# Banded attention: the softmax division moved behind the value products, and cached K and V loaded without a staging copy

## The chip, the cores and the metric

The kernel runs on one core of a Trainium2 chip. The metric is the device time of one execution in microseconds. The core has five engines that run side by side: TensorE (PE in the profile; its weight loads are shown apart as PEld), VectorE (DVE), ScalarE (ACT), GpSimd (POOL) and SyncE (SP), which issues most of the transfers. Transfers (DMAs) run on 16 engines of their own. A matmul writes into PSUM, a memory of eight banks, and DVE or ACT carries the result from there into SBUF.

## The reference

One layer of a hybrid encoder on 2048 tokens of 1024 features, all in float32. A norm and one combined projection give, among others, q, k and v of eight heads of 64 columns. Attention is banded: tokens go in chunks of 64, and a chunk sees itself and the eight chunks before it, with a learned bias by distance:

```python
scores = jnp.einsum('bnqhd,bnkhd->bnhqk', qc, kb).astype(jnp.float32) * (d ** -0.5)
...
scores = jnp.where(valid[None, :, None, None, :], scores + bias[None, None], NEG_INF)
p = jax.nn.softmax(scores, axis=-1)
out = jnp.einsum('bnhqk,bnkhd->bnqhd', p.astype(vb.dtype), vb)
```

Beside it runs a recurrent branch (RWKV-7). Both branches are projected (`proj_a`, `proj_b`), gated, added, projected once more (`w_out`), normed and added to x. A feed-forward part with a squared ReLU follows. The change concerns the attention alone.

## The kernel before, in words

The tokens go through in four groups of 512 (`G`). For each group `run` (L1206) does three stages: the recurrent branch (`phase_rwkv`), the attention (`phase_attention`, L884) and the merge (`phase_merge`, L935), in which gates, branches and `w_out` come together. The feed-forward part follows after all four groups.

Float32 products are made from halves: `split` (L68) rounds a tensor to the reduced format F32R on ACT (`hi`) and takes the remainder on DVE (`lo`), and `mm3` (L72) sums hi·hi, hi·lo and lo·hi. `dense` (L82) does so for a projection of 128 columns: load 512 KB of weights (L62, on SP's queue), split them, 24 matmuls of 512 columns into a PSUM tile `psd`.

`att_pair` (L756) handles two heads at a time, four pairs to a group. It makes q, k and v by three calls of `dense`. Keys stand in `KK`, values in `VV`; each holds two groups of tokens, the group before in half 0 and the own in half 1, since the band reaches back 512 tokens. The own half is stored to device memory (L797, L798) and read again one group later: from the second group on, `kr` and `vr` are loaded (L764, L767) into one staging buffer of their own, and ACT copies them into half 0 of `KK` and `VV` (L765, L768).

Then for each head of the pair (`par`), each half of the 512 queries (`half`) and each 128 queries of that (`b`, number `qb`), one score block:

- PE: scores of 128 queries and up to 640 keys into `ps_s` (L820);
- DVE: add the bias and take the extreme `mn` of each row (L826);
- ACT: exponential of the row, its sum into `sm` (L831; the reading of the sum is an instruction of its own);
- DVE: reciprocal of the sum (L833), and the row multiplied by it (L834);
- PE: up to five transposes of 128x128 into `ps_pt` (L838);
- ACT and DVE: the transposed block split into `PTh` and `PTl` (L842, L843).

After two blocks PE multiplies with the values into a PSUM tile `ps_pv` of 256 columns (L850, 12 matmuls where the whole band exists). The hi and lo parts of V's columns come out on the lower and upper 64 rows; ACT copies the upper rows to `y2` (L852) and DVE adds both into `ya` (L853). When both heads are through, `ya` (128 columns of features by 512 queries) is split into `self.ya` (L856), which the merge multiplies with `proj_a`.

`ps_s` and `ps_pt` have one buffer each of two PSUM banks, `ps_pv` two of one bank each, `psd` two. `KK` and `VV` have two buffers, so that the next pair's projections can be made while this pair's blocks run.

After the four pairs `load_y` (L914) reads the recurrent branch's result, and `branch(y, 1, i)` (L923, called at L908) multiplies it with `proj_b`, gates it (L932) and stores it; the merge does the same with `proj_a`.

The source's order isn't that of the engines. The framework places instructions on each engine by a plan of its own, made when the program is built: what is ready goes first, and among ready ones what stands earlier in the source. On each engine, and on SP's queue of transfers, the order is then fixed. In the trace PE so alternates between score blocks of one pair, projections `psd` of the next, and, in the last pair, the `proj_b` products `ps_p`.

## Time and profile before

| what | value |
|---|---|
| time, median of 3 runs (lowest to highest) | 3462.41 us (3460.87 to 3465.66) |
| time of the profiled execution | 3462.33 us |
| its span, first to last instruction | 3460.6 us |
| mean granted clock of TensorE | 0.985 |
| instructions | 50793 |
| DMA share, 16 engines: main queue | 40.2% |

The profile names an instruction by its line in the kernel, its engine, its operation, and the tiles written and read ("out<-in"). Busy time counts an engine's instructions without overlap twice. A matmul's duration is longer than the step from one to the next, as matmuls are pipelined. "Idle before" is the idle time of an engine just before the instructions of a group, and what ended it. Times in a timeline count from the first instruction.

The attention stages in this execution lie at about 318 to 434, 803 to 950, 1339 to 1486 and 1875 to 2021 us (from the first projections that only attention uses to the last value product); the merges follow each. The first group has no group before it, so its stage has fewer keys, and no `kr` and `vr`.

### The profile page before, as it was taken

The numbers are of one execution on the slowest core, as the hardware profiler recorded it, in microseconds if no ns is written. First come the engines' busy times: TensorE is split into PE (matmuls) and PEld (weight loads), VectorE is DVE, ScalarE is ACT, GpSimd is POOL, SyncE is SP. The second block draws the span as 40 slices with busy tenths as digits, with TensorE's granted clock in tenths as the row PEclk, the third lists the DMA queues.
The fourth block names the chain that finished last, engine by engine and source line by source line (L and its number), as shares of the span: only waits on it lengthen the run. The fifth ranks groups of instructions, "written<-read, shape, count | busy, mean of one in ns | idle before, by whom it ended". The sixth has DMA issues, their size and how long they took to land. (4 is left out here: it accounts for less than half of the span.)

```text
span 3460.6 us, 50793 instructions
## 1 busy us (share of the span) xinstructions
PE 3310.7 (96%) x19233; PEld 2677.4 (77%) x19233; DVE 2421.3 (70%) x4206; ACT 1429.6 (41%) x2399; POOL 352.7 (10%) x700
## 2 busy tenths in 40 slices
PE   7999999999998999999999979999999999999998
PEld 5777777777877777877777867888888878888886
DVE  5774856766856765865774875777887788766667
ACT  4434634436644445644435635333331143331112
POOL 2210002100003110002210000111100021100001
PEclk9999999999999999999999999999999999999999
DMA  5223453225365225365224277334845374343333
GB/s 147 82 86 125 130 182 119 62 89 186 111 223 161 62 92 159 122 226 163 82 86 134 81 232 254 125 120 143 271 175 188 109 239 129 113 152 98 98 98 110
DMA packets 430124, 481.14 MB, mean 139 GB/s; under 512 B 19564, under 2 KB 322864, under 8 KB 429880
## 3 DMA queue, kind: packets, MB, share of 16 engines
q1 hardware_dynamic: 419640, 444.34, 40.2%
q0 software_dynamic: 10240, 33.56, 2.6%
q8 instruction: 151, 2.47, 0.3%
q14 instruction: 93, 0.76, 0.1%
HBM read 356.16 MB, written 124.81 MB: 139 GB/s over the span
## 5 line engine op out<-in xcount | busy, mean ns | idle before, releaser
L78 PE MATMUL ps_dn<-fop 128*128 128x512 f32 x3072 | 700.1, 390 | 0.9 <-DVE u L1169 0.9
L78 PEld LDWEIGHTS ps_dn<-fop 128*128 128x128 f32 x3072 | 575.9, 188 | 121.3 <-DVE u L1169 1.3
L78 PE MATMUL psd<-hh,whi 128*128 128x512 f32 x1344 | 546.4, 407 | 16.7 <-ACT whi L69 13.5
L78 PE MATMUL psd<-hl,whi 128*128 128x512 f32 x1344 | 544.9, 405 | 0.0
L78 PE MATMUL psd<-hh,wlo 128*128 128x512 f32 x1344 | 541.4, 403 | 0.7 <-DVE wlo L70 0.5
L69 ACT CAST whi<-wraw 128x1024 fp32r<-128x1024 f32 (+1 forms) x296 | 255.6, 864 | 578.2 <-PE psd L78 392.3
L70 DVE TENSOR_TENSOR wlo<-wraw,whi 128x1024 fp32r<-128x1024 f32 (+1 forms) x296 | 292.6, 989 | 264.9 <-ACT whi L69 200.4
L1169 DVE TENSOR_TENSOR u<-u,ps_dn 128x512 f32<-128x512 f32 x480 | 322.5, 684 | 152.8 <-PE ps_dn L78 152.0
L78 PEld LDWEIGHTS psd<-hh,whi 128*128 128x128 f32 x1344 | 258.3, 192 | 71.7 <-ACT whi L69 15.5
L78 PEld LDWEIGHTS psd<-hh,wlo 128*128 128x128 f32 x1344 | 258.0, 192 | 52.5 <-DVE wlo L70 3.5
L78 PEld LDWEIGHTS psd<-hl,whi 128*128 128x128 f32 x1344 | 258.6, 192 | 48.8
L69 ACT CAST fop<-wdraw 128x1024 fp32r<-128x1024 f32 x64 | 67.1, 1049 | 427.5 <-DVE u L1169 321.9
L1090 POOL DMA_DIRECT2D ad<-r x128 | 69.4, 543 | 683.8 <-DVE r L1089 683.8
L78 PE MATMUL ps_p<-yh,whi 128*128 128x512 f32 x256 | 107.8, 421 | 29.8 <-DVE th L932 17.8
L69 ACT CAST s12h<-s 128x1024 fp32r<-128x1024 f32 x32 | 33.7, 1054 | 185.1 <-PE ps_u L78 185.1
L826 DVE CUSTOM_DVE_ANT_0 sc<-bias,ps_s 128x640 f32<-128x640 f32 (+4 forms) x128 | 93.3, 729 | 22.4 <-PE ps_pt L838 13.0
L831 ACT ACTIVATE sc<-sc,mn 128x640 f32<-128x640 f32 (+4 forms) x128 | 97.8, 764 | 22.4 <-DVE mn L826 21.7
L78 PE MATMUL ps_p<-yh,wlo 128*128 128x512 f32 x256 | 105.4, 412 | 1.6 <-DVE wlo L70 1.6
L959 PE MATMUL ps_o<-whi,mh 128*128 128x512 f32 x256 | 98.6, 399 | 7.7 <-ACT whi L69 6.8
L78 PE MATMUL ps_p<-yl,whi 128*128 128x512 f32 x256 | 105.3, 412 | 0.0
L843 DVE TENSOR_TENSOR PTl<-ps_pt,PTh 128x640 fp32r<-128x640 f32 (+4 forms) x128 | 94.1, 735 | 12.9 <-ACT PTh L842 12.2
L959 PE MATMUL ps_o<-wlo,mh 128*128 128x512 f32 x256 | 102.1, 399 | 1.1 <-DVE wlo L70 1.1
(345 smaller groups left out, 6566.9 us busy)
## 6 DMA issues: line engine op xcount, KB each, us to landing
wraw<-in_w_in_dram SPq DMA_DIRECT2D x168, 512.0 KB
wraw<-in_w_up_dram SPq DMA_DIRECT2D x80, 512.0 KB
ad<-r POOLq DMA_DIRECT2D x128, 256.0 KB, 2.5
wdraw<-in_w_down_dram SPq DMA_DIRECT2D x64, 512.0 KB
araw<-ad SPq DMA_DIRECT2D x64, 512.0 KB
gd<-gate SPq DMA_DIRECT2D x64, 256.0 KB
th<-gd SPq DMA_DIRECT2D x64, 256.0 KB
wraw<-in_w_out_dram SPq DMA_DIRECT2D x64, 256.0 KB
```

Of the source, the lines that this page charges most:

```text
L69: self.nc.scalar.copy(hi, src)
L70: self.nc.vector.tensor_tensor(lo, src, hi.bitcast(F32), ALU.subtract)
L78: mm = nc.tensor.matmul(ps, l, r, start=n == 0, stop=n == last).ins
L826: nc.vector.tensor_tensor_reduce(sc[:, 0:n], bias[:, s0:640], pss[:, c0 : c0 + n], 1.0, 3.0e38, ALU.add, ALU.min, mn,)
L831: nc.scalar.activation(sc[:, 0:n], sc[:, 0:n], AF.Exp, scale=-1.0, bias=mn, accum_out=sm)
L843: nc.vector.tensor_tensor(lv, pst[:, 0:nk], hv.bitcast(F32), ALU.subtract)
L959: nc.tensor.matmul(ps[t], l[:, k, ts], r[:, 0], start=k == 0 and j == 0, stop=k == KB - 1 and j == 2)
L1090: nc.gpsimd.dma_start(self.ad[fb][:, th], r)
L1169: nc.vector.tensor_tensor(u[t][:, ns], u[t][:, ns], ps, ALU.add)
```

## The change

Three things are done. The cached K and V are loaded straight into half 0 of `KK` and `VV`. The exponentials are transposed and multiplied with V as they are, and their sums are kept, one column for each head and block, in a tile `sm` of 128x8 for a pair. And a new function `finish` divides at the end: reciprocal of the eight columns, a transpose to 8x128 (`ps_rt`), a copy to `rt`, four matmuls with a constant 0/1 matrix `place` that spread each query's two factors over the 64 rows of their heads (`ps_rb`, 128x512), a product with `ya`, and the split. `finish` of a pair stands in the source behind the next pair's projections; that of the last pair stands behind `load_y`. `ps_pv` becomes 512 columns wide, so `y2` and `ya` are made once for a head instead of twice.

```diff
         if not first:
-            kr = ap.tile([P, 2, G], F32, tag="kr", bufs=1, name="kr")
-            nc.sync.dma_start(kr, self.kc[p])
-            nc.scalar.copy(KK[:, :, 0], kr)
-            vr = ap.tile([P, GT, 2, 2, C], F32, tag="kr", bufs=1, name="vr")
-            nc.sync.dma_start(vr, self.vc[p])
-            nc.scalar.copy(VV[:, 0], vr)
+            nc.sync.dma_start(KK[:, :, 0].bitcast(F32), self.kc[p])
+            nc.sync.dma_start(VV[:, 0].bitcast(F32), self.vc[p])
...
+        self.finish(p - 1)
         ya = ap.tile([P, G], F32, tag="ya", name="ya")
+        sm = ap.tile([P, 2 * GT], F32, tag="sm", name="sm")
+        self.unscaled[p] = ya, sm
         for par in range(2):
+            pv = self.pv.tile([P, 2, 2 * P], F32, tag="pv", name="ps_pv")
...
-                    sm = ap.tile([P, 1], F32, tag="sm", bufs=4, name="sm")
-                    nc.scalar.activation(sc[:, 0:n], sc[:, 0:n], AF.Exp, scale=-1.0, bias=mn, accum_out=sm)
-                    rs = ap.tile([P, 1], F32, tag="rs", bufs=4, name="rs")
-                    nc.vector.reciprocal(rs, sm)
-                    nc.vector.tensor_scalar(sc[:, 0:n], sc[:, 0:n], rs, None, ALU.mult)
+                    col = par * GT + qb
+                    nc.scalar.activation(
+                        sc[:, 0:n], sc[:, 0:n], AF.Exp, scale=-1.0, bias=mn, accum_out=sm[:, col : col + 1]
+                    )
...
-                pv = self.pv.tile([P, 2 * P], F32, tag="pv", name="ps_pv")
...
-                    nc.tensor.matmul(pv, st, x[:, kt], start=i == 0, stop=i == len(terms) - 1)
-                y2 = ap.tile([C, 2 * P], F32, tag="y2", name="y2")
-                nc.scalar.copy(y2, pv[C:P])
-                nc.vector.tensor_tensor(
-                    ya[rows[par], half * 2 * P : (half + 1) * 2 * P], pv[0:C], y2, ALU.add
-                )
+                    nc.tensor.matmul(pv[:, half], st, x[:, kt], start=i == 0, stop=i == len(terms) - 1)
+            pvf = pv.rearrange("p h q -> p (h q)")
+            y2 = ap.tile([C, G], F32, tag="y2", bufs=1, name="y2")
+            nc.scalar.copy(y2, pvf[C:P])
+            nc.vector.tensor_tensor(ya[rows[par]], pvf[0:C], y2, ALU.add)
+
+    def finish(self, p):
+        if p < 0:
+            return
+        nc, ap = self.nc, self.ap
+        ya, sm = self.unscaled.pop(p)
+        nc.vector.reciprocal(sm, sm)
+        ps = self.pv.tile([P, G], F32, tag="pv", name="ps_rt")
+        nc.tensor.transpose(ps[0 : 2 * GT, 0:P], sm, self.ident)
+        rt = ap.tile([2 * GT, P], F32, tag="rt", name="rt")
+        nc.scalar.copy(rt, ps[0 : 2 * GT, 0:P])
+        ps = self.pv.tile([P, G], F32, tag="pv", name="ps_rb")
+        for qb in range(GT):
+            nc.tensor.matmul(ps[:, qb * P : (qb + 1) * P], self.place[:, qb], rt, start=True, stop=True)
+        nc.vector.tensor_tensor(ya, ya, ps, ALU.mult)
         self.split(self.ya[0][:, p], self.ya[1][:, p], ya)
...
+            self.place = pp.tile([2 * GT, GT, P], F32, name="place")
+            nc.gpsimd.memset(self.place, 1.0)
+            pl = self.place.rearrange("e q (h d) -> e q h d", d=C)
+            nc.gpsimd.affine_select(
+                pl, pl, [[-1, GT], [-GT, 2], [0, C]], ALU.is_equal, 0.0, base=0, channel_multiplier=1
+            )
+            self.unscaled = {}
             for p in range(NP):
                 self.att_pair(g, p)
             y = self.load_y(pp, self.ap)
+            self.finish(NP - 1)
```

## The prediction

> **What bounds the kernel now.** I read the page first (engine totals), then the table of busy time by stretch (the four attention stages, each followed by its merge, and a stretch of the feed-forward part), then who waited for whom on PE in one attention stage, the groups of instructions, and the timeline for single steps.

> The page, section 1:

> ```profile
> PE 3310.7 (96%) x19233; PEld 2677.4 (77%) x19233; DVE 2421.3 (70%) x4206; ACT 1429.6 (41%) x2399; POOL 352.7 (10%) x700
> ```

> PE is busy for 96% of the span, so a step off PE can only buy what PE idles. The table by stretch; columns are the stretch, its length, then busy time (instructions) of PE, PEld, DVE, ACT and POOL, granted clock, DMA share, GB/s:

> ```profile
> 318.00:434.00 116.00, 113.47 (x582) 87.80 (x581) 91.40 (x244) 74.49 (x179) 2.55 (x16) 1.00 0.46 148
> 434.00:520.00 86.00, 80.76 (x355) 64.58 (x355) 45.66 (x68) 34.89 (x60) 4.11 (x10) 0.98 0.56 177
> 803.00:950.00 147.00, 143.51 (x826) 118.48 (x825) 119.41 (x244) 99.16 (x188) 2.33 (x16) 1.00 0.45 147
> 950.00:1038.00 88.00, 80.82 (x350) 63.53 (x349) 48.38 (x70) 36.37 (x64) 7.17 (x13) 0.98 0.70 224
> 1339.00:1486.00 147.00, 143.01 (x822) 118.01 (x821) 119.41 (x244) 98.91 (x187) 2.50 (x16) 1.00 0.45 146
> 1486.00:1575.00 89.00, 81.51 (x354) 64.21 (x353) 48.77 (x70) 36.68 (x65) 6.45 (x13) 0.98 0.67 222
> 1875.00:2021.00 146.00, 143.19 (x825) 118.57 (x824) 119.28 (x244) 98.83 (x187) 2.34 (x16) 1.00 0.37 119
> 2021.00:2123.00 102.00, 81.75 (x320) 62.95 (x319) 53.95 (x77) 32.02 (x49) 0.00 (x0) 0.92 0.79 252
> ```

> The attention stages are the rows at 318, 803, 1339 and 1875. There PE idles 116 - 113.47 = 2.5, 3.5, 4.0 and 2.8 us: 12.8 us in all. DVE is at 81% and ACT at 67%; neither ends anything for long, because whenever a score block waits, PE is given a projection of the next pair (psd) or, in the last pair, a product with proj_b (ps_p). **PE bounds the attention stages**; the merges behind them are bound by transfers as much as by PE (DMA share 0.56 to 0.79, PE idle 5 to 20 us). Who PE waited for in the stage 803 to 950 (waiting place, releaser, us, times, longest):

> ```profile
> PE ps_vt L791 <- ACT vf L788: 0.9, 1, 0.9
> PE ps_pv L850 <- ACT PTh L842: 0.9, 4, 0.3
> PE psd L78 <- ACT KK L784: 0.8, 1, 0.8
> PE ps_pt L838 <- DVE VV L795: 0.6, 1, 0.6
> ```

> No row names the two DVE operations that the change removes.

> **The change part by part.** The groups that it touches, or that stand for what it adds (busy us, mean ns of one | idle before):

> ```profile
> L833 DVE RECIPROCAL rs<-sm 128x1 f32<-128x1 f32 x128 | 20.4, 159 | 15.8 <-ACT sc L831 14.2
> L834 DVE TENSOR_SCALAR sc<-sc,rs 128x640 f32<-128x640 f32 (+4 forms) x128 | 64.8, 507 | 2.1
> L765 ACT CAST KK<-kr 128x1024 fp32r<-128x1024 f32 x12 | 12.6, 1050 | 4.2 <-DMA kr<-kc 4.0
> L768 ACT CAST VV<-vr 128x1024 fp32r<-128x1024 f32 x12 | 12.6, 1053 | 5.0 <-DMA vr<-vc 4.8
> L852 ACT COPY y<-ps_pv 64x256 f32<-64x256 f32 x64 | 23.5, 368 | 44.8 <-PE ps_pv L850 44.2
> L853 DVE TENSOR_TENSOR ya<-ps_pv,y 64x256 f32<-64x256 f32 x64 | 26.6, 416 | 13.1 <-ACT y L852 12.1
> L784 ACT CAST KK<-psd 64x512 fp32r<-64x512 f32 x32 | 18.5, 578 | 4.4 <-PE psd L78 3.5 <-DVE KK L785 0.5
> L785 DVE TENSOR_TENSOR KK<-psd,KK 64x512 fp32r<-64x512 f32 x32 | 22.0, 688 | 5.3 <-ACT KK L784 4.5
> L794 ACT CAST VV<-ps_vt 128x128 fp32r<-128x128 f32 x64 | 16.7, 260 | 9.0 <-DVE VV L795 8.1 <-PE ps_vt L791 0.7
> L932 DVE SCALAR_TENSOR_TENSOR th<-th,ps_p 128x512 f32<-128x512 f32 x64 | 43.7, 682 | 25.0 <-DMA th<-gd 12.9 <-PE ps_p L78 12.0
> L838 PE MATMUL ps_pt<-ident,sc 128*128 128x128 f32 x560 | 82.8, 274 | 2.1 <-DVE VV L795 1.2 <-DVE sc L834 0.3
> L438 PE MATMUL ps_v<-cmat,v 128*128 128x128 f32 x128 | 17.7, 281 | 0.2
> ```

> *DVE.* Removed: 128 reciprocals and 128 scalings, 20.4 + 64.8 = 85.2 us. The 64 additions of the halves (26.6 us) become 32 of 64x512, as L785: 32 x 0.69 = 22.0. Added per pair: one reciprocal of 128x8 (0.16, as L833) and one product of 128x512 with PSUM (0.68, as L932): 16 x 0.84 = 13.4. Net -76 us, some 19 a stage. *ACT.* Removed: 24 casts, 25.2 us. The 64 y copies (23.5) become 32 at 0.58 (as L784): 18.5. Added: 16 copies of 8x128 (0.26, as L794): 4.2. Net -26 us. On a PE-bound stage none of this is on the path, except where an idle time of PE stands behind it.

> *PE.* Nothing is removed: transposes, score and value products keep their number and shape. Per pair `finish` adds a transpose (128 columns of the identity) and four full-f32 matmuls of 128 columns. Their price is PE's step from one to the next, not the mean duration, since they overlap. Timeline of PE (start, us, engine, line, ...):

> ```profile
> 67.80 1.05 PE L438 MATMUL ps_v<-cmat,v 128*128 128x128 f32 x8
> ...
> 844.00 0.40 PE L78 MATMUL psd<-hl,whi 128*128 128x512 f32 x1
> 844.24 0.71 PE L838 MATMUL ps_pt<-ident,sc 128*128 128x128 f32 x5
> 844.70 0.48 PE L78 MATMUL psd<-hh,wlo 128*128 128x512 f32 x1
> 845.02 0.40 PE L78 MATMUL psd<-hh,whi 128*128 128x512 f32 x1
> ...
> 845.48 0.39 PE L78 MATMUL psd<-hh,wlo 128*128 128x512 f32 x1
> 845.78 0.39 PE L850 MATMUL ps_pv<-PTh,VV 128*128 128x256 f32 x1
> ```

> A transpose steps by (0.71 - 0.27) / 4 = 0.11. L438 is a full-f32 matmul of the same size as the new ones, and it has **two records to a matmul**: 16 calls (four groups of tokens, four pairs) of 4 make 64, and the row counts 128; L838, a transpose, has one (560 calls, x560). One record steps by (1.05 - 0.28) / 7 = 0.11, so a matmul by 0.22. Per pair 0.11 + 4 x 0.22 = 0.99, for 16 pairs **15.8 us**. The transpose and the four products are also two new places where PE changes to work that has just become ready: from 845.48 to 845.78 such a change took 0.30 in place of the 0.23 that psd steps by, 0.07 more; 32 x 0.07 = **2.2 us**. The bounds of that are 0 (844.00 to 844.24: nothing) and 0.9 once a pair (the vt row above: PE stood while ACT copied vf, just as it would for the copy of the transposed sums), 14.4.

> *What PE gets back.* Of the four waits, KK ends before the first score block and stays. PTh is a copy that stays; with ACT emptier I take half, 0.4. The vt wait (0.9) stood behind a cast of L768 and goes; the pt wait (0.6) stood behind a full DVE and goes. That is 1.9 of 3.5 us in each of the three stages with cached K and V and about 1 in the first: **-7 us**. Bounds: 0, and all 12.8 us plus as much again in waits that the rows hide, since a psd matmul counts 0.39 for a step of 0.23: -25.6.

> *The merge.* In the last pair a score block costs DVE 0.16 + 0.51 less, so its 8 blocks end some 5 us sooner and two proj_b products of 12 matmuls (12 x 0.23 = 2.8 us) fall out of the attention stage into the merge. Their PE time is only moved, but the merge runs its PE at 80 to 94%: some 10% of 2 x 2.8 us in four merges, **+2 us** (0 to 4). The tail of the last pair gets longer by a product (0.68) and by wider copies (0.2 + 0.3); it stays hidden behind the proj_b products still left, and would cost 1.2 us a stage if they were gone.

> *Loads in place.* The same 24 loads of 512 KB, now into KK and VV with two buffers. K's load must wait on SP's queue until the pair before last has made its last scores, and weight, bias and gate loads are queued behind it; the K projection writes the same buffer and had this wait already. I take 0 and give the rest to a rival. The POOL work for `place` comes once a stage, where POOL is busy 2 of 147 us: 0. `finish` issues no DMA.

> **Sum**, on the profiled execution of 3462.3 us (span 3460.6; the median of the runs is 3462.4, so the same figure serves): 3462.3 + 15.8 + 2.2 - 7 + 2 = 3475.3. I forecast **3475 us**, slower by 0.37%.

> **Rivals.**
> 1. *Faster: the shorter chain pays.* Mechanism: in each score block the transposes no longer wait for reciprocal and scaling, DVE falls from 81% to some 68%, and PE stops losing steps between blocks. For it: every visible and as many hidden waits could go, 3462.3 + 15.8 - 25.6 = **3452**. It decides once PE regains over 25 us, 6 a stage, against 3.5 seen idle. Against it: no wait row names L833 or L834, and L838's idle before is 2.1 us in the whole run. [...] So this rival gets 0.14.
> 2. *It cancels.* All 12.8 visible us go and the merge loses nothing: 3462.3 + 18.0 - 12.8 = **3467.5**, within 0.2%. Chance 0.17.
> 3. *Worse: a new wait.* PE stands for the transposed sums, or the weights stand behind K's load on SP, by 0.9 us a pair as in the vt row: 16 x 0.9 = 14.4 in place of 2.2: **3487**. For it: the last merge shows what late weights cost, in PE's waits there:

> ```profile
> PE ps_p L78 <- ACT whi L69: 11.7, 2, 6.1
> PE ps_o L959 <- ACT whi L69: 4.1, 2, 2.8
> ```

>    Against it: in the attention stages other PE work is always ready. Chance 0.13.

> That the loads in place do nothing is no rival: what was stored is already in the rounded form, and 24 casts simply go.

> **How the numbers follow.** Forecast 0.56, rivals 0.14, 0.17 and 0.13. About 0.2% (6.9 us) is what a measurement of this kernel can tell from no change. Slower by more: 0.56 + 0.13 = 0.69; within: 0.17; faster: 0.14. The range reaches from rival 1 to beyond rival 3: 3452 to 3490.

> **What would show it.** In the profile after: PE with 16 x 9 more records, all in the attention stages, and the four L438-like matmuls stepping by 0.22; DVE busy down by about 76 us, ACT by 26; attention stages longer by some 2 to 3 us each with PE idle there down to about 6 us in all. I am wrong if the attention stages get shorter (PE was losing more than its rows show), if the copy of the sums stops PE for about 1 us a pair, or if the merges change by more than 3 us each.

## The result, and the profile after

The changed kernel takes 3473.86 us (median, 3468.93 to 3478.89), the kernel before 3462.87 us on the same chip (3458.81 to 3469.59), 11 runs each: a ratio of **1.0028, 95% interval 1.0018 to 1.0037**. The profiled execution took 3473.86 us as well, with a span of 3472.2 us against 3460.6. Page of after, engine totals:

```profile
PE 3323.0 (96%) x19377; PEld 2691.1 (78%) x19377; DVE 2362.3 (68%) x3950; ACT 1407.1 (41%) x2359; POOL 358.8 (10%) x708
```

PE has 144 more records, 16 x 9 as worked out. DVE's groups changed by what the prediction said (the removed ones 85.2 us, `ya` 26.6 to 21.9, 11.0 and 3.2 added); its busy time fell by 59 only, since busy time counts what overlaps once. The table by stretch of after, attention and merge in turn (columns as before):

```profile
318.00:435.00 117.00, 114.26 (x602) 89.98 (x601) 79.30 (x176) 72.67 (x174) 3.62 (x20) 1.00 0.43 140
435.00:527.00 92.00, 84.95 (x371) 68.07 (x370) 48.65 (x72) 35.70 (x61) 3.55 (x10) 0.96 0.54 175
810.00:960.00 150.00, 146.36 (x850) 121.50 (x849) 100.17 (x177) 90.35 (x174) 2.92 (x17) 0.99 0.43 142
960.00:1052.00 92.00, 82.94 (x365) 64.90 (x364) 54.70 (x76) 40.28 (x70) 8.88 (x18) 1.00 0.70 236
1346.00:1494.00 148.00, 145.27 (x852) 120.86 (x851) 100.08 (x177) 90.69 (x174) 3.08 (x18) 1.00 0.44 144
1494.00:1587.00 93.00, 84.06 (x363) 65.69 (x362) 54.81 (x76) 40.28 (x69) 8.76 (x18) 0.98 0.70 234
1879.00:2029.00 150.00, 146.42 (x849) 121.39 (x848) 100.42 (x177) 90.33 (x174) 3.01 (x17) 0.99 0.35 114
2029.00:2134.00 105.00, 84.33 (x329) 65.24 (x328) 56.17 (x80) 32.46 (x49) 0.00 (x0) 0.90 0.77 246
```

DVE has some 19 us less to do in each full attention stage (119.41 to 100.17), and the stage got longer all the same. PE still idles 2.7 to 3.6 us in each, 12.6 us in all where it was 12.8. But the idle time is another one. Who PE waited for from 810 to 960 us, all rows:

```profile
PE ps_s L820 <- DMA KK<-kc: 3.4, 1, 3.4
```

The four waits of before are gone, and **one new wait** stands in their place: the first scores of the stage wait for the cached K, loaded straight into `KK`. In the other two stages with cached K it is 2.5 and 3.3 us, 9.2 in all. The timeline of SP's queue in after has the load, that of PE the scores:

```profile
812.11 0.59 SPq L763 DMA_DIRECT2D KK<-kc  x1
```

```profile
818.23 0.39 PE L820 MATMUL ps_s<-KK,QA 128*128 128x320 f32 x1 [3.40 <-DMA KK<-kc]
```

The stage's first copy of q is at 810.16, so these scores come 8.1 us behind it. Before, with a load issued just as early behind that copy (804.91 and 803.10), they came 11.0 us behind it, with projections right up to them and no wait:

```profile
804.91 0.57 SPq L764 DMA_DIRECT2D kr<-kc  x1
```

```profile
813.89 0.39 PE L78 MATMUL psd<-hh,wlo 128*128 128x512 f32 x1
814.12 0.30 PE L820 MATMUL ps_s<-KK,QA 128*128 128x320 f32 x1
```

So the load isn't issued later, but the scores stand some 3 us sooner in PE's order: 19 projection matmuls `psd` lie between that copy and them, where before 43 do, a whole projection of 24 more. There they wait for the transfer; they start 6.1 us behind its issue, while before ACT's copy out of `kr` started 4.8 us behind it (809.75). Not all of the wait is the transfer's, though. The same scores need the group's own keys, and DVE ends its half of these for the first head 1.5 us into the wait, at 815.64 + 0.69 = 816.33:

```profile
815.64 0.69 DVE L781 TENSOR_TENSOR KK<-psd,KK 64x512 fp32r<-64x512 f32 x1
```

In the three stages that makes 4.5 of the 9.2 us that the scores would wait at this place even if K lay there already. The wait leaves a trace behind it; the stretch around it in after:

```profile
812.00:818.00 6.00, 2.83 (x13) 2.02 (x11) 4.49 (x7) 3.30 (x5) 0.00 (x0) 1.00 0.84 264
818.00:823.00 5.00, 4.77 (x15) 3.85 (x16) 0.43 (x1) 0.00 (x0) 0.59 (x4) 0.66 1.04 388
823.00:828.00 5.00, 4.87 (x25) 3.80 (x24) 1.72 (x3) 2.26 (x3) 0.00 (x0) 1.00 0.49 160
```

PE is busy for 2.83 of 6 us, and in the 5 us behind that its granted clock is 0.66: the wait is paid a second time, with 5 x 0.34 = 1.7 us (behind the 2.5 us of the third group the clock stays at 1.00). Then the groups and the timeline of `finish` in after:

```profile
L868 PE MATMUL ps_rb<-rt,place 8*128 8x128 f32 x128 | 18.7, 284 | 0.0
```

```profile
860.75 0.66 PE L787 MATMUL ps_vt<-ident,vf 128*128 128x128 f32 x4
861.34 1.15 PE L868 MATMUL ps_rb<-rt,place 8*128 8x128 f32 x8
862.42 0.41 PE L820 MATMUL ps_s<-KK,QA 128*128 128x320 f32 x1
```

The four products take 862.42 - 861.34 = 1.08 us of PE, in 8 records, and PE doesn't wait ahead of them.

**Where the time went.** I cut every execution at the same places: the first copy of q in a group (QA), the last value product, the last proj product `ps_p`, and the last w_out product `ps_o`. "Attention" runs from the first to the second, "proj" to the third, "w_out" to the fourth, "recurrent" from there to the next group's QA. Sums over the four groups in us, and the recurrent stages of the last two groups by themselves (up to the first QA it is 318 us, the recurrent stage of the second group 283 to 286, and behind the last w_out product 1338 to 1341, in all kernels). The column behind them says how much of these two stages is idle time of PE, and how much PE lost, while it was busy, because only half its clock was granted. One execution of each kernel is behind a row, and executions of one kernel differ by up to 18 us, so differences of a few us between rows are not certain:

| kernel | attention | proj | w_out | recurrent, group 3 and 4 | of these, idle + half clock | end |
|---|---|---|---|---|---|---|
| before | 554.3 | 176.4 | 188.5 | 301.1 + 300.7 | 34.9 + 19.7 | 3460.6 |
| after | 563.6 | 191.8 | 189.8 | 294.9 + 292.6 | 29.3 + 9.8 | 3472.2 |
| e1, after with loads staged | 566.7 | 194.2 | 188.8 | 297.1 + 293.2 | 28.6 + 14.2 | 3480.9 |
| e2, before with loads in place | 553.8 | 174.9 | 189.8 | 293.0 + 295.0 | 28.5 + 11.6 | 3446.5 |
| e3, undivided, staged, no finish | 546.5 | 187.8 | 189.0 | 294.1 + 295.9 | 31.2 + 12.4 | 3453.3 |
| e4, staged, finish by transposes | 584.4 | 154.2 | 196.2 | 307.7 + 308.6 | 51.9 + 16.0 | 3494.6 |
| e5, after without finish | 544.6 | 182.1 | 188.7 | 292.2 + 293.3 | 28.8 + 8.3 | 3441.7 |
| e6, place products twice in a burst | 580.2 | 220.5 | 184.7 | 293.8 + 293.7 | 31.5 + 9.8 | 3513.6 |
| e7, before, tiles at all steps | 555.1 | 178.0 | 196.9 | 300.1 + 298.8 | 38.0 + 16.9 | 3469.8 |
| e8, e2 with tiles at all steps | 554.1 | 173.2 | 199.3 | 291.2 + 291.1 | 24.9 + 15.7 | 3451.0 |
| e9, finish without its PE steps | 542.4 | 181.5 | 186.7 | 303.0 + 301.0 | 38.6 + 18.0 | 3454.9 |
| e10, place products twice, apart | 573.8 | 210.2 | 188.3 | 293.0 + 293.3 | 28.4 + 9.8 | 3500.9 |
| e11, no finish for the last pair | 557.5 | 182.9 | 188.8 | 293.4 + 292.3 | 28.7 + 8.3 | 3455.4 |
| e12, before, norm tiles earlier | 555.3 | 174.9 | 190.3 | 296.2 + 293.1 | 28.5 + 13.1 | 3449.9 |

From before to after, attention and proj lose 24.7 us (730.7 to 755.4), and 14.3 come back in two recurrent stages (601.8 to 587.5), **whose code the change doesn't touch**. What happens there is seen at their start, behind the last w_out product. First 46 us of the third group's stage, before and then after:

```profile
1038.00:1084.00 46.00, 38.21 (x166) 30.09 (x164) 27.25 (x29) 27.07 (x45) 12.31 (x32) 0.89 0.67 217
```

```profile
1052.00:1098.00 46.00, 41.17 (x195) 33.10 (x194) 28.04 (x34) 26.51 (x44) 15.84 (x33) 0.96 0.60 189
```

After gets 195 matmuls through where before gets 166. The place where the residual tiles' transposes stand, in the trace of before and of after (last columns: first and last start):

```profile
L995 PE MATMUL ps_ht<-ident,xn x32: 271/272/331, 1038.2 to 1063.6; 128*128 128x128 f32 x32
```

```profile
L1018 PE MATMUL ps_ht<-ident,xn x32: 270/273/417, 1051.8 to 1072.9; 128*128 128x128 f32 x32
```

There are four tiles of `residuals` in both. Before, they come about 8 us apart over 25.4 us, and the last norm tile stands 18 matmuls ahead of the end of w_out; after, the plan has put the last of the norm tiles 171 matmuls ahead, two residual tiles come at once, and the last starts after 21.1 us. Who PE waited for in the stage, before and then after (two rows each):

```profile
PE ps_ht L995 <- DVE xn L990: 3.9, 2, 2.0
PE psd L78 <- ACT whi L69: 3.7, 1, 3.7
```

```profile
PE psd L78 <- ACT whi L69: 2.4, 1, 2.4
PE ps_ht L1018 <- DVE xn L1013: 2.4, 2, 1.7
```

The third and fourth group's recurrent stages as a whole, before and then after:

```profile
1038.00:1339.00 301.00, 283.38 (x2258) 224.39 (x2257) 192.75 (x390) 130.76 (x225) 53.30 (x99) 0.97 0.34 106
1575.00:1875.00 300.00, 282.76 (x2256) 224.03 (x2255) 192.56 (x390) 130.29 (x225) 52.62 (x99) 0.96 0.34 106
```

```profile
1052.00:1346.00 294.00, 279.32 (x2254) 222.04 (x2253) 188.49 (x386) 128.17 (x220) 52.42 (x95) 0.98 0.33 102
1587.00:1879.00 292.00, 277.39 (x2256) 220.09 (x2255) 188.47 (x386) 128.41 (x220) 52.51 (x96) 0.99 0.33 103
```

PE idles less there, and is granted more of its clock. The two together are the whole difference, and of the 14.3 us the clock is the larger part (19.7 to 9.8). With idle time and half clock taken off, the two stages last 546 to 549 us in before, after and ten of the twelve experiments; in e7 and e8, which have residual tiles in w_out, 544 and 542.

### The profile page after: what moved, and what is told of

Its sections match the earlier page's. It is cut to its first block, busy times and chain, and to the rows that moved or that the text cites. A ratio compares the mean times of both kernels' runs of the same rounds, so it can differ in the third digit from the quotient of the medians.

```text
span 3472.2 us, 50833 instructions
## 1 busy us (share of the span) xinstructions
PE 3323.0 (96%) x19377; PEld 2691.1 (78%) x19377; DVE 2362.3 (68%) x3950; ACT 1407.1 (41%) x2359; POOL 358.8 (10%) x708
## 5 line engine op out<-in xcount | busy, mean ns | idle before, releaser
L78 PE MATMUL ps_dn<-fop 128*128 128x512 f32 x3072 | 700.0, 390 | 0.9 <-DVE u L1192 0.9
L78 PEld LDWEIGHTS ps_dn<-fop 128*128 128x128 f32 x3072 | 575.9, 188 | 121.3 <-DVE u L1192 1.3
L78 PE MATMUL psd<-hh,whi 128*128 128x512 f32 x1344 | 544.7, 405 | 12.6 <-ACT whi L69 11.4
L78 PE MATMUL psd<-hl,whi 128*128 128x512 f32 x1344 | 544.8, 405 | 0.0
L78 PE MATMUL psd<-hh,wlo 128*128 128x512 f32 x1344 | 540.1, 402 | 0.6 <-DVE wlo L70 0.5
L69 ACT CAST whi<-wraw 128x1024 fp32r<-128x1024 f32 (+1 forms) x296 | 255.3, 863 | 594.0 <-PE psd L78 379.8
L70 DVE TENSOR_TENSOR wlo<-wraw,whi 128x1024 fp32r<-128x1024 f32 (+1 forms) x296 | 293.7, 993 | 246.0 <-ACT whi L69 179.9
L78 PEld LDWEIGHTS psd<-hh,whi 128*128 128x128 f32 x1344 | 257.3, 191 | 66.5 <-ACT whi L69 13.0
L78 PEld LDWEIGHTS psd<-hh,wlo 128*128 128x128 f32 x1344 | 257.7, 192 | 51.4 <-DVE wlo L70 2.7
L78 PEld LDWEIGHTS psd<-hl,whi 128*128 128x128 f32 x1344 | 257.6, 192 | 48.6
L69 ACT CAST fop<-wdraw 128x1024 fp32r<-128x1024 f32 x64 | 67.1, 1048 | 426.9 <-DVE u L1192 304.0
L78 PE MATMUL ps_p<-yh,whi 128*128 128x512 f32 x256 | 108.6, 424 | 30.7 <-DVE th L955 18.7
L841 ACT CAST PTh<-ps_pt 128x640 fp32r<-128x640 f32 (+4 forms) x128 | 80.0, 625 | 72.2 <-PE ps_pt L837 69.7
L831 ACT ACTIVATE sc<-sc,mn 128x640 f32<-128x640 f32 (+4 forms) x128 | 97.7, 763 | 28.3 <-DVE mn L826 27.2
L69 ACT CAST s12h<-s 128x1024 fp32r<-128x1024 f32 x32 | 33.8, 1055 | 184.0 <-PE ps_u L78 184.0
L78 PE MATMUL ps_p<-yh,wlo 128*128 128x512 f32 x256 | 105.5, 412 | 0.0
L78 PE MATMUL ps_p<-yl,whi 128*128 128x512 f32 x256 | 105.5, 412 | 0.0
L842 DVE TENSOR_TENSOR PTl<-ps_pt,PTh 128x640 fp32r<-128x640 f32 (+4 forms) x128 | 94.3, 737 | 16.0 <-ACT PTh L841 15.2
```

What stands on the lines that cost most here:

```text
L69: self.nc.scalar.copy(hi, src)
L70: self.nc.vector.tensor_tensor(lo, src, hi.bitcast(F32), ALU.subtract)
L78: mm = nc.tensor.matmul(ps, l, r, start=n == 0, stop=n == last).ins
L831: nc.scalar.activation(sc[:, 0:n], sc[:, 0:n], AF.Exp, scale=-1.0, bias=mn, accum_out=sm[:, col : col + 1])
L841: nc.scalar.copy(hv, pst[:, 0:nk])
L842: nc.vector.tensor_tensor(lv, pst[:, 0:nk], hv.bitcast(F32), ALU.subtract)
```

## The experiments

Letters: A is always that PE pays for the steps that `finish` puts on it; each text says what it is set against (B in the first four: that the load in place, with its wait, is what the change costs). Ratios are to the kernel before on the same chip.

**e1: the changed kernel with the loads staged again**, in halves, and `rt` with one buffer, for room.

```diff
-            nc.sync.dma_start(KK[:, :, 0].bitcast(F32), self.kc[p])
-            nc.sync.dma_start(VV[:, 0].bitcast(F32), self.vc[p])
+            for h in range(2):
+                kr = ap.tile([P, G], F32, tag="kr", bufs=1, name="kr")
+                nc.sync.dma_start(kr, self.kc[p][:, h])
+                nc.scalar.copy(KK[:, h, 0], kr)
+            ... (V likewise, in two halves)
...
-        rt = ap.tile([2 * GT, P], F32, tag="rt", name="rt")
+        rt = ap.tile([2 * GT, P], F32, tag="rt", bufs=1, name="rt")
```

> The changed kernel, but cached K and V go through a staging buffer and ACT again (in halves of 256 KB, since a buffer of 512 KB no longer fits beside the constant matrix). Theory A (the prediction's): PE bounds the attention and pays 16 to 18 us for finish, of which 7 to 10 come back from DVE and ACT; loading in place is worth about nothing, so this takes what the changed kernel takes, 3473 us within 3. Theory B: what costs is a new wait, the first scores of a stage for K loaded in place (3.4, 2.5 and 3.3 us of PE in the three stages, and some 5 us at a granted clock of 0.66 behind each, 1.7 us more): without it 3473.9 - 9.2 - 5.1 = 3460 us, no slower than the kernel before.

1.0045 (1.003 to 1.0061). Not faster than the changed kernel (the two intervals overlap), so the load in place doesn't cost anything in sum; B falls, and A's number is missed too. With staging, the first scores wait 2.3 to 2.4 us for ACT's copy of K in place of the load. They stand as early as in the changed kernel, 19 `psd` behind the first copy of q, so it isn't the missing copy alone that moves them; kernels that stage K whole (before, e3, e4, e7, e12) have 43. What the plan goes by is not shown.

**e2: the kernel before with the loads in place**, nothing else (the reverse of e1's edit, on the kernel before).

> The kernel before with the loads in place alone. Theory A: 24 casts fewer on ACT, no PE work moved: 3463 us within 3, or up to 3 faster. Theory B: the new wait appears here too: 9 to 14 us slower than before, 3472 to 3477, with a row in PE's waits that names the transfer into KK.

0.9943 (0.993 to 0.9957): faster by 18 us at the median, which neither theory had. This is the fastest kernel here that still computes the whole layer. B's new wait does appear, 2.8, 2.3 and 2.3 us ahead of the first scores (two of the three rows name ACT's cast of the group's own keys, which ended within 0.1 us of the landing), but PE's idle time over the four attention stages stays at 12.7 us (12.8 before): the wait takes the place of earlier ones. And the stage table says that attention and proj gained 2.0 us only (730.7 to 728.7); 13.8 are in the two recurrent stages, as less idle time and less half clock.

**e3: the kernel before, undivided**, so its output is never divided by the sums.

```diff
-                    rs = ap.tile([P, 1], F32, tag="rs", bufs=4, name="rs")
-                    nc.vector.reciprocal(rs, sm)
-                    nc.vector.tensor_scalar(sc[:, 0:n], sc[:, 0:n], rs, None, ALU.mult)
```

> The kernel before without reciprocal and scaling in the score blocks and with nothing in their place (the outputs of the attention stay undivided; staging as before). It bounds what taking DVE's two operations off the chain is worth. Theories A and B: only PE's waits in the attention stages come back, 7 to 12.8 us: 3450 to 3456. Rival C (PE loses much more than its rows show, and the shorter chain gives it back): 20 us or more, 3443 or less.

0.9965 (0.9953 to 0.9978), as expected in size. 85 us of DVE shorten the attention by 7.8 us, and 5.0 of these are products with `proj_b` that fall out of it into proj (the stage holds 239 proj matmuls in place of 260), so that 2.8 us are gained. PE's idle time in the four stages goes from 12.8 to 11.6 us. Proj gets 11.4 longer, through these products and through norm tiles (their transposes there rise from 20.7 to 34.0 us). The recurrent stages fall by 11.8. So the right number came about in another way than thought.

**e4: the changed kernel, staged (whole, as before), with `finish` by transposes**: the inverted sums are spread over 128x512 on DVE, into the one buffer that `vf` has, and four transposes take the place of transpose, copy and the four products.

```diff
+        nc.vector.reciprocal(rx, sm.rearrange("p (h q) -> p q h", q=GT)[:, :, :, None].to_broadcast((P, GT, 2, C)))
...
-            nc.tensor.matmul(ps[:, qb * P : (qb + 1) * P], self.place[:, qb], rt, start=True, stop=True)
+            nc.tensor.transpose(ps[:, qb * P : (qb + 1) * P], rx[:, qb].rearrange("p h d -> p (h d)"), self.ident)
```

> The changed kernel with staging as before, and finish cheaper on PE: DVE writes the inverted sums spread over 64 columns a head, and four transposes of 128x128 put them in place (4 x 0.11 us for a pair in place of 0.11 + 4 x 0.22; no copy of the transposed sums, no constant matrix). Theory A: 9 us less PE work than the changed kernel: 3465 us. Theory B: 3460 - 9 = 3451 us, faster than before.

1.0096 (1.0081 to 1.0111), missed by all. 80 records of PE fewer than e1, attention and proj 22.3 us shorter (738.6 against 760.9; 17.0 of it norm transposes that have moved out into later stages), and slower by 13.7 us of span: w_out loses 7.4 and the recurrent stages 26.0. This pointed to the order of the tiles between the attentions. What of it comes from the shared buffer isn't told apart.

**e5: the changed kernel without `finish`'s arithmetic** (reciprocal, transpose, copy, products and the product with `ya` left out; the output isn't divided).

```diff
-        nc.vector.reciprocal(sm, sm)
-        ... (transpose, rt, the four products, ya times ps)
         self.split(self.ya[0][:, p], self.ya[1][:, p], ya)
```

> The changed kernel without finish's arithmetic: reciprocal, transpose, copy, the four products with the 0/1 matrix and the product with ya are left out, so the attention's output is not divided by the sums; loads stay in place, everything else stays. Theory A (PE bounds the attention stages, so finish costs what PE steps through: 16 x 1.1 us): 3474 - 17.6 = 3456, within 3452 to 3460. Theory B (finish is filled into idle time of PE, and the slowdown comes from the other order of the plan): 3470 to 3476.

0.9937 (0.9925 to 0.995). `finish` costs (1.0028 - 0.9937) x 3468 = 31.6 us; A's 17.6 is too small, and B falls. Attention and proj: 726.7 against 755.4, 28.7 us. The stage 804 to 949 of e5:

```profile
804.00:949.00 145.00, 141.64 (x817) 117.79 (x816) 98.09 (x171) 89.57 (x171) 2.95 (x21) 0.99 0.45 147
```

**e6: the four products twice**, the second time over the first.

```diff
             nc.tensor.matmul(ps[:, qb * P : (qb + 1) * P], self.place[:, qb], rt, start=True, stop=True)
+            nc.tensor.matmul(ps[:, qb * P : (qb + 1) * P], self.place[:, qb], rt, start=True, stop=True)
```

> The changed kernel with each of the four products with the 0/1 matrix made twice (the second overwrites the first with the same values). Theory A: 64 more full-f32 matmuls of 128 columns at 2 x 0.112 us step = 14.3 us on the path: 3488, within 3484 to 3492. Theory B: they fall into idle time: 3472 to 3478.

1.0132 (1.0119 to 1.0146): 36 us more than the changed kernel, 41 in the span, for 14.4 us of records (a burst takes 1.98 us in place of 1.08). A alone doesn't give that. The table by stretch of e6, two of the bursts (they start at 869.53 and 906.60), each with the time behind it:

```profile
869.00:871.50 2.50, 2.50 (x21) 2.22 (x20) 2.17 (x6) 1.79 (x6) 0.00 (x0) 1.00 0.04 11
871.50:875.00 3.50, 3.50 (x11) 3.00 (x11) 2.63 (x7) 1.97 (x5) 0.00 (x0) 0.55 0.61 191
...
906.00:908.60 2.60, 2.60 (x22) 2.30 (x21) 1.87 (x5) 1.70 (x6) 0.00 (x0) 1.00 0.04 14
908.60:912.00 3.40, 3.40 (x12) 2.84 (x12) 2.43 (x6) 1.70 (x4) 0.00 (x0) 0.61 0.43 147
```

PE is busy all the time, and its clock still falls to about half behind the burst. That follows 10 of the 16 bursts here; behind the bursts of 1.08 us in the changed kernel the clock stays at 1.00. Span and mean granted clock of the changed kernel and of e6:

```profile
core 0: 3472.2 us, clock 0.987
```

```profile
core 0: 3513.6 us, clock 0.978
```

(1 - 0.987) x 3472 = 45 us and (1 - 0.978) x 3514 = 77 us of clock weren't granted, 32 us more. 23.8 of these lie in attention and proj (42.6 against 18.8 us); with 16.6 us by which the products' own steps grew, they cover 40.4 of the 45.3 us that attention and proj gained.

**e7: the kernel before with the tiles of norm and residuals between all steps** of the second half of w_out.

```diff
-                    if n == 1 and k % 2 == 0:
+                    if n == 1:
```

> The kernel before with one line of the merge changed, the attention untouched: the tiles of the norm and of the residuals are put between all eight steps of the second half of w_out, not between every second one. Theory C (what the changed kernel wins back in the starts of the recurrent stages comes from the place of these tiles alone): the four residual tiles stand behind the last w_out product at 8 us each in two groups; with one or two of them moved into the merge 6 to 8 us a group go: 3466 - 13 = 3453, within 3448 to 3458. Rival D (they are bound by transfers, and cost the same wherever they stand): 3463 to 3469.

1.0006 (0.9997 to 1.0015): no difference, as rival D said. The recurrent stages fell by 2.9 us and w_out rose by 8.4. This edit made a third order, though (norm tile 70 matmuls ahead of the end, two residual tiles inside w_out), not that of the changed kernel, so it doesn't settle C.

**e8: e2 with the same edit.**

> The kernel before with the loads in place and the same line of the merge changed: both parts that cost PE nothing, without the undivided exponentials and finish. Theory C: 3448 less what is left of the tiles behind w_out (two groups, one more tile each moved in, some 4 to 6 us a group): 3438, within 3434 to 3443. Rival D: 3446 to 3450.

0.9953 (0.9939 to 0.9967): not better than e2 (0.9943). Three residual tiles in w_out cost it 9.5 us there and save 5.7 in the recurrent stages. C's number falls; D's holds but for 3 us.

**e9: `finish` without its PE steps** (transpose, copy and products left out; `ya` is multiplied by one column of the inverted sums, so the scale is wrong).

```diff
-        ps = self.pv.tile([P, G], F32, tag="pv", name="ps_rt")
-        ... (transpose, rt, the four products)
-        nc.vector.tensor_tensor(ya, ya, ps, ALU.mult)
+        nc.vector.tensor_scalar(ya, ya, sm[:, 0:1], None, ALU.mult)
```

> The changed kernel with finish's steps on PE and the copy rt left out: the reciprocal stays, and ya is multiplied by one column of the inverted sums, so the output is scaled by wrong factors. Without finish the changed kernel took 0.9937 of the kernel before, with it 1.0028. Theory A (the price of finish is PE's: its records, the steps around them, and what they push out of the stage): 0.9937 to 0.996, 3446 to 3454. Rival E (the price is the tail: reciprocal, product and split of ya stand between the last value product and the first product with proj_a): at least half of the 31 us stays, 0.998 to 1.0028, 3461 to 3478.

0.9975 (0.9963 to 0.9986), between the two. The stage table separates them: attention and proj are 723.9 us, even 2.8 below e5, so **the tail costs nothing and `finish`'s price is that of PE's steps** (with ACT's copy between them, which e9 leaves out too), E falls. The 13.2 us by which e9's span exceeds e5's come from the recurrent stages (604.0 against 585.5). Its plan has the norm tile 18 matmuls ahead of the end again, as the kernel before; first 46 us of the stage, e9 and then e5:

```profile
1036.00:1082.00 46.00, 36.89 (x155) 28.96 (x154) 26.05 (x28) 26.12 (x44) 12.37 (x32) 0.89 0.66 214
```

```profile
1037.00:1083.00 46.00, 41.37 (x202) 32.77 (x201) 28.64 (x35) 27.59 (x46) 15.88 (x33) 1.00 0.62 196
```

**e10: the products twice, in a burst of their own** at the second head of pairs 1 to 3.

```diff
+            if par and p:
+                ps = self.pv.tile([P, G], F32, tag="pv", name="ps_again")
+                for qb in range(GT):
+                    nc.tensor.matmul(
+                        ps[:, qb * P : (qb + 1) * P], self.place[:, qb], self.again, start=True, stop=True
+                    )
+                rs = ap.tile([P, 1], F32, tag="rs", bufs=1, name="rs")
+                nc.vector.tensor_copy(rs, ps[:, 0:1])
```

> The changed kernel with the four products with the 0/1 matrix made a second time, as in the run before, but in another place: a burst of their own at the second head of pairs 1 to 3, 12 bursts in all, written to a PSUM tile of which only one column is copied away. Together in one burst the doubled products cost 36 to 41 us for 14.4 us of records, and the granted clock fell to half for some 3.4 us behind 10 of 16 bursts. Theory F (PE's clock falls behind a stretch of about 2 us in which PE runs only these small products; 1 us is too short for it): 12 x 1.05 = 12.6 us and no more dips in the attention stages than in the changed kernel, ratio to the kernel before 1.0028 + 0.0036 = 1.0064, within 1.005 to 1.008. Rival G (each full-f32 product of this kind costs 0.56 us, twice its records, wherever it stands): 48 x 0.56 = 27 us, ratio 1.0106, within 1.0095 to 1.012.

1.0087 (1.0073 to 1.0101), between F and G. F's sign is there: no burst is followed by a fall of the clock, and in the full stages it is granted almost whole, against 0.97 in e6. Stage of e10, then of e6:

```profile
816.00:967.00 151.00, 148.33 (x865) 122.45 (x864) 98.96 (x178) 90.17 (x174) 2.56 (x17) 1.00 0.42 135
```

```profile
819.00:973.00 154.00, 150.82 (x867) 125.05 (x867) 98.98 (x175) 90.02 (x173) 2.71 (x17) 0.97 0.41 133
```

But the price is 28.7 us of span (28.6 in attention and proj) and not 12.6. Summing PE's steps (each matmul's start to the next one's) by tile, 15.9 of it are the 96 new records, 1.33 us a burst, since they are strewn between others; 10.7 are proj products: all 764 of them take 230.6 us in place of 219.9, as 31 have moved from the stage into the merge. These 10.7 are no work of PE's: 5.1 are idle time and 5.6 half clock in the merges.

**e11: `finish` for pairs 0 to 2 only**; the last pair's outputs stay undivided.

```diff
-            self.finish(NP - 1)
+            ya, _ = self.unscaled.pop(NP - 1)
+            self.split(self.ya[0][:, NP - 1], self.ya[1][:, NP - 1], ya)
```

> The changed kernel with finish for pairs 0 to 2 of each group; the last pair's outputs stay undivided. Theory A with an equal price for each pair: 31 / 4 = 8 us less than the changed kernel, ratio 1.0028 - 0.0023 = 1.0005, within 0.9995 to 1.0013. Rival E (the last pair's finish stands alone between the attention and proj_a and carries most of the price): 16 us or more less, ratio 0.998 or below.

0.9991 (0.9981 to 1.0001), between the two again. By attention and proj (e5 726.7, e11 740.4, after 755.4): the twelve `finish` of pairs 0 to 2 cost 13.7 us, **1.14 us each**; the four of the last pairs 15.0 us, **3.75 us each**. The profiled execution of e11 is its fastest, though, 6.8 us below its median; by the ratios (0.9937, 0.9991, 1.0028) it is 18.7 and 12.8 us, 1.6 and 3.2 each. The last pair's is the dearer either way, by how much is open.

**e12: the kernel before with the norm tiles given out earlier**, which gives the order of the changed kernel to the residual tiles.

```diff
-                    if n == 1 and k % 2 == 0:
+                    if n == 0 and k % 2 == 0:
```

> The kernel before with one condition of the merge changed (the tiles of the next norm and of the residuals are given out between the steps of the first half of w_out instead of the second), everything else untouched. The last norm tile then stands 114 matmuls ahead of the last w_out product instead of 18, and the residual tiles behind it as in the changed kernel (two at once, then 40 and 25 matmuls later, instead of four evenly spread). Theory C (the recurrent stages of the third and fourth group start 6 to 9 us sooner in that order, whatever the attention does): these two stages fall from 602 to 588 us, ratio to the kernel before 0.9960, within 0.995 to 0.9972. Rival D (what such an order wins there it loses in w_out or in the products ahead of it, as in the run with the tiles between all steps): 0.9985 to 1.0015.

0.9963 (0.9949 to 0.9976): C as expected, D falls. Attention and proj stay (730.2 against 730.7), w_out gets 1.8 longer, the recurrent stages fall from 601.8 to 589.3, half by idle time (34.9 to 28.5) and half by clock (19.7 to 13.1). Its residual tiles and the first 46 us:

```profile
L995 PE MATMUL ps_ht<-ident,xn x32: 271/273/447, 1039.0 to 1060.0; 128*128 128x128 f32 x32
```

```profile
1036.00:1082.00 46.00, 41.96 (x189) 33.83 (x188) 26.42 (x31) 28.30 (x45) 12.23 (x30) 0.93 0.63 200
```

Two tiles at once, 189 matmuls in place of 166, with no other edit. It isn't one lucky execution: the mean granted clock of e12's five runs is 0.987 to 0.989, that of the kernel before beside them 0.983 to 0.987. So one line of the merge gives 13 us without touching the attention, and two versions, e2 and e12, beat both kernels for the same reason.

## Why the prediction came out as it did

The forecast, 3475 us, was near the measured 3473.86. In its sum the prices of PE's new records and of the merge were about right; what PE gets back was not, and the order of other tiles was not in it. These two cancelled, and that is luck. PE's steps from a group's first QA to its last proj product, summed by tile as in e10, before to after: 729.9 to 754.6 us.

- **PE bounds the attention stages: right.** e3 takes 85 us off DVE and the stages lose 7.8, of which 5.0 are products that moved on. Rival 1, which needed over 25 us regained, is not borne out.
- **Price of `finish`, 15.8 + 2.2 = 18.0:** the steps measure 17.9 for `ps_rt` and `ps_rb`, and 2.6 more at the step from the value transposes (`ps_vt`, 6.1 to 8.7): 20.5. The two records to a product and the step of 0.22 held. Taken away whole (e5, e9), it is worth 29 to 32 us. For pairs 0 to 2 the sum's 1.13 a pair is near what e11 shows (1.14 by stages, 1.6 by medians). The last pair's is where the step was too small: "stays hidden behind the proj_b products still left". Between e11 and after, its own records take 4.6 of 15.0. Proj products take 7.3 more for the same number of them: 5.1 of that is idle time (the wait for DVE's gating, `th`, rises from 4.8 to 8.6 us) and 2.2 half clock. 4.3 lie in the projections `psd`, where PE idles 2.7 more, mostly ahead of the first scores, and loses 1.7 to the clock. So what the last pair's `finish` adds beyond its records is waiting and the clock falls that go with it.
- **"-7", what PE gets back: the step that failed.** e3 takes the same work off DVE, leaves the loads staged, and gets 2.8 us back; PE's idle time, forecast to fall to about 6 us in all, is 11.6 in e3 and 12.6 in the changed kernel. The waits that the prediction named did go: without the new wait 3.4 us of idle time are left in after, the steps of `psd` are unchanged at 267.4 though 9.2 us of new wait are in them, and `ps_pt`, `ps_pv` and `ps_s` lose 1.6. That is some 10.8 regained and 9.2 paid back at another place, -1.6 in the net.
- **"Loads in place: 0": right as a net price, wrong in its reason.** e2 has them alone, and attention and proj come out 2.0 us shorter. But "the K projection writes the same buffer and had this wait already" looks at the buffer, and not at where the plan puts what reads it: the first scores stand 3 us sooner in PE's order, ahead of the end of the transfer, with 9.2 us of wait in three stages and a half clock behind it in two. It isn't rival 3 (weights behind K's load): the weights go ahead of it on SP (issued at 811.68, the load at 812.11).
- **The merge, "+2": right in size, with luck in it.** 43 proj matmuls fell from the stage into the merge, not the 4 x 24 reckoned with, and all proj products together take 219.9 us in place of 217.4, +2.5. Idle time among them grew by 1.7 and half clock by 2.4; their other steps fell.
- **Not foreseen: -9.9 us by the order of tiles nobody edited.** Norm tiles pulled into proj cost 3.3 (`pstr` and the first `ps_o`), and the recurrent stages and w_out give back 13.2. The prediction treated the plan's order outside the attention as fixed. e12 against before shows what this order is worth by itself, 12.5 us in two recurrent stages; e9 against e5, which differ in `finish` too, have 18.5 there.

20.5 - 1.6 + 2.5 - 9.9 = 11.5, within 0.1 of the difference of the spans; the forecast had 18.0 - 7 + 2 = 13.0. The rise of 0.3% is thus real, but as a price of the idea it is too small: with loads and residual tiles alike, as in e2, undividing and `finish` cost 26.7 us of attention and proj (728.7 to 755.4, of which 5.1 is half clock), and some 29 us by the ratios (0.9943 to 1.0028).

Of the signs named: the records and the step of 0.22 came; attention grew by 1.0, 3.5, 0.4 and 4.5 us; PE's idle time didn't fall to 6 us, since the wait for K took the place; and the merges (proj and w_out) grew by 3.0 to 6.2 us each, which had been named as what would make it wrong.

## What to carry to other kernels

Where one engine is busy for 96%, work taken off the others buys little: 85 us of DVE were worth 2.8 us here. New work on that engine can cost more than its own steps, 29 to 32 us for 20.5 here, once it pushes other work into a stage that waits anyway. Where a planner fixes the order, compare stages that the edit doesn't touch as well: here an edit in the attention moved tiles in the merge, worth nearly as much as the whole measured change, and a one-line change of order gave more than the edit cost. A stage that changes without being edited should be read by the busiest engine's idle time and granted clock first. A number that comes out right should still be taken apart by stages: here a wait and an order of 9 us each stood behind it, neither in the sum.

## What the hardware showed unexpectedly

PE's clock fell in steps of one size: 3.41 us at half, or a multiple of it (6.83 and 10.24 us in before and after; the last fall reaches past the last instruction), with 1.7 us lost for each step. It did so behind a wait of PE, as here in before, where PE is busy for 1.56 of 4 us:

```profile
975.00:979.00 4.00, 1.56 (x11) 1.14 (x10) 2.60 (x5) 3.59 (x8) 0.98 (x4) 1.00 0.99 328
979.00:983.00 4.00, 3.87 (x10) 3.11 (x11) 3.58 (x6) 0.62 (x1) 0.99 (x1) 0.58 0.71 241
```

And it fell behind PE's own work, e6's 1.98 us of full-f32 products with 8 rows, with PE busy throughout. Here too it went with what one window holds: ten of the eleven windows with 1.73 us or more of these products were followed by a fall, and none with less, as where a burst lies across two windows, or in e10, whose bursts are mixed with other products. No run tells the few rows from the data type.
